# Odd layer of a two-layer decoder trunk: attention stores issued from ScalarE's queue, the merges' loads from GpSimd's

## The chip, the cores and the metric

The program runs on one core of one Trainium2 chip. The metric is the device time of one execution in microseconds, as the median of several runs; lower is better. In the profile the engines are PE (TensorE matmul), PEld (its weight loads), DVE (VectorE), ACT (ScalarE), POOL (GpSimd) and SP (SyncE). A row such as SPq, ACTq or POOLq belongs to the instruction queue of that engine: a wait, or the issue of a DMA.

## What is computed

The reference is a trunk of two residual layers over 1024 tokens of width 1024, each followed by a gated feed-forward block with a short convolution. The first layer mixes tokens by a gated delta rule and by pooling. The second one, the odd layer, is the one at hand: attention in three groups, each with eight heads of 128 channels, and each group looking back over another dilation.

```python
DIL_PATTERNS = ((128, 1), (512, 4), (2048, 16))
def odd_mixer(h, w_in, w_out, q_norm, k_norm):
    for gi, (window, dil) in enumerate(DIL_PATTERNS):
        proj = (h @ cols).reshape(B, T, 3, ATT_HEADS, ATT_DH)
        q = rms_norm(proj[:, :, 0], q_norm) * (ATT_DH ** -0.5)
        k = rms_norm(proj[:, :, 1], k_norm)
        o, lse = dilated_band_attention(q, k, proj[:, :, 2], dil, window // dil, slopes)
    wts = jax.nn.softmax(jnp.stack(lses), axis=0)
    o = jnp.sum(wts[..., None] * jnp.stack(outs), axis=0)
    return o.reshape(B, T, ATT_W) @ w_out
```

So each head has three outputs, one of each group, and they are merged by weights that come from the three softmax denominators. The merged heads are then multiplied by the output matrix.

## The kernel before, in words

All matmuls of weights are done in three passes: a weight and an activation are each split into a high part (whi, hh, oh) and a low part (wlo, hl, ol), and three products are summed in PSUM. A weight is loaded as a granule of 128 x 512 floats into a tile `raw` (4 buffers) from the sync queue at L190; ACT copies it to `whi` and another engine subtracts to get `wlo` (L185 and L186; 9 buffers of each). The subtraction runs on DVE in most of the odd layer, and on GpSimd after `lo_eng` is set back, which is ahead of the output projection.

The odd layer is written as two streams. `dense()` is the projections: for each of 12 pairs of heads (`todo`: a group g and a head pair hp) it multiplies by eight granules of q and k weights, in four blocks of 256 tokens, and, for every second pair, by eight granules of v weights. `v` goes to DRAM and comes back by strides: the stores (L1495) and loads (L1463, L1466, L1469) are issued from GpSimd. Behind the last pair it does the output projection, `update()` over two pairs of rows of the output matrix (L212 to L214 on TensorE, then L249 on DVE, which adds into the residual tile `xr`), and the first steps of the next stage.

`chains()` is everything with a chain of dependences: `attend(i)` for each pair, and `merge(hp)`. `weave()` puts them between the dense matmuls, some 1.3 to 3.5 us of dense matmuls after each step. The order of the code is a priority, and a scheduler at build time lays out each engine's queue from it; on the chip each engine's queue then runs in that order, and an instruction that waits holds up all behind it on the same queue.

In `attend(i)` a unit is a block of 256 tokens and one head: scores (PE, L1550), bias and maximum (DVE, L1562, L1566 or L1570, L1573), exponential (ACT, L1575), transposes (PE, L1583), their copy out of PSUM (ACT L1587 or DVE L1585 in turn), the product with v (PE, L1594), and the copy of the result into `stg` (ACT, L1596). After every second unit two DMAs store `stg` into the group's DRAM tensor `os` (L1600), 130 KB each: 96 in all.

In `merge(hp)`, `load(t)` brings 128 tokens of two heads from the three groups into `ld` (L1630, three DMAs of 130 KB, 3 buffers of `ld`), computes weights (DVE and ACT, L1632 to L1640) and mixes (ACT L1645, DVE L1647): 96 DMAs in all. `turn_o` transposes (PE, L1653); for hp 0 and 1 ACT copies the tile out (L1657) and two DMAs store it to `osp2` (L1659, 16 in all), from where it comes back later as a granule; for hp 2 and 3 it is split where it is.

L1600, L1630 and L1659 stand on the sync queue, beside the weights (L190), the reload of the residual tiles (`xr<-xs`, L424) and of `osp2` (L456).

Of the kernel before, what the change touches and what calls it, by code (L numbers as in the profile page):

```python
# [17 lines left out]
P = 128  # L18
# [16 lines left out]
def trunk(ctx, tc, x, c, ada_w, ada_b, norm_mix, norm_ffn, ev_w_in, ev_w_out, gdn_conv_w,  # L35
          gdn_a_log, gdn_dt_bias, gdn_norm, pool_w, pool_scale, od_w_in, od_w_out,
          att_q_norm, att_k_norm, ffn_w_up, ffn_conv_w, ffn_conv_b, ffn_w_down, out):
    nc = tc.nc
# [373 lines left out]
    osp2 = dram.tile([4, P, T], F32, name="osp2")  # L412
# [921 lines left out]
    def odd(xt, h, vec, acc):  # L1334
# [5 lines left out]
        with tc.tile_pool(name="po", bufs=1) as po:  # L1340
# [189 lines left out]
            def attend(i, need):  # L1530
# [58 lines left out]
                def values(n):  # L1589
                    b2, hh = un[n]  # L1590
                    ps = s_ps()
                    for j, (ks, a0, m) in enumerate(spans[n][0]):
                        for c, kb in enumerate(ks):
                            nc.tensor.matmul(ps[:, j * P:(j + 1) * P], pTs[n][:, a0 + c * P:a0 + (c + 1) * P],  # L1594
                                             vb(kb, hh), start=(c == 0), stop=(c == len(ks) - 1))
                    nc.scalar.copy(stg[b2][:, :, hh, 0:P], ps[:, :256].rearrange("p (a f) -> p a f", a=2))  # L1596
                    if hh:
                        for j in range(2):
                            rows = tok_rows(osc[g], g, b2 * 2 + j)
                            nc.sync.dma_start(rows[:, hp * 2:hp * 2 + 2, :], stg[b2][:, j])  # L1600

                for n in range(9):
                    if n < 8:
# [11 lines left out]
            def merge(hp, need):  # L1615
# [11 lines left out]
                def load(t):  # L1627
                    ld = et("ld", 3, (P, 3, 2, 130))
                    for g in range(3):
                        nc.sync.dma_start(ld[:, g], osc[g][t * P:(t + 1) * P, hp * 2:hp * 2 + 2, :])  # L1630
                    mx, e, dn = et("mx", 2, (P, 1, 2)), et("me", 2, (P, 3, 2)), et("dn", 2, (P, 3, 2))
                    nc.vector.tensor_reduce(out=mx[:, 0, :], in_=ld[:, :, :, 128].rearrange("p g x -> p x g"),  # L1632
                                            axis=mybir.AxisListType.X, op=ALU.max)
                    nc.vector.tensor_tensor(out=e, in0=ld[:, :, :, 128], in1=mx.to_broadcast([P, 3, 2]), op=ALU.subtract)
                    nc.scalar.activation(e, e, AF.Exp)
                    nc.vector.tensor_tensor(out=dn, in0=e, in1=ld[:, :, :, 129], op=ALU.mult)
                    nc.vector.tensor_reduce(out=mx[:, 0, :], in_=dn.rearrange("p g x -> p x g"),
                                            axis=mybir.AxisListType.X, op=ALU.add)
                    nc.vector.reciprocal(mx, mx)
                    nc.vector.tensor_tensor(out=e, in0=e, in1=mx.to_broadcast([P, 3, 2]), op=ALU.mult)  # L1640
                    if t % 2 == 0:
                        mos[t // 2] = t2k()
                    for hh in range(2):
                        m = blk4(mos[t // 2])[hh * 2 + t % 2]
                        nc.scalar.activation(m, ld[:, 0, hh, 0:P], AF.Copy, scale=e[:, 0, hh:hh + 1])  # L1645
                        for g in (1, 2):
                            nc.vector.scalar_tensor_tensor(out=m, in0=ld[:, g, hh, 0:P], scalar=e[:, g, hh:hh + 1],  # L1647
                                                           in1=m, op0=ALU.mult, op1=ALU.add)

                def turn_o(t2):  # L1650
# [4 lines left out]
                    if hp < 2:  # L1655
                        og = t2k()
                        nc.scalar.copy(og, ps)  # L1657
                        for hh in range(2):
                            nc.sync.dma_start(osp2[hp * 2 + hh][:, s], og[:, hh * 256:(hh + 1) * 256])  # L1659
                        return  # L1660
                    for hh in range(2):
                        split(o[hh][0][:, s], o[hh][1][:, s], ps[:, hh * 256:(hh + 1) * 256], nc.vector)
# [112 lines left out]
```

## Time and profile before

| | us |
|---|---|
| median of 3 runs | 3056.04 (3054.67 to 3056.47) |
| the profiled execution | 3055.07 |
| its span, first to last instruction | 3053.3 |
| TensorE busy in the span | 2965.5 (97%) |
| VectorE / ScalarE / GpSimd busy | 1938.5 / 1125.9 / 996.0 |

The span is 1.75 us shorter than the time of the same execution. The odd layer's attention runs from about 1311 us to 2300 us of the span. A row of the stretches gives, for a piece of the span, its length and then the busy time of PE, PEld, DVE, ACT and POOL (with the number of instructions), the granted clock, the mean busy share of the 16 DMA engines and the GB/s that they moved; the difference between its length and TensorE's busy time is what TensorE stood still, and the granted clock tells how much of the time it had its full rate (1.00 is 2.4 GHz, 0.50 is 1.2 GHz). A row of the waits says which instruction waited, for which one, how long in all, how many times, and how long the longest.

### The profile page before, as it was taken

What the parts mean: (1) busy time and instruction counts of PE and PEld (TensorE: products, weight loads), DVE (VectorE), ACT (ScalarE), POOL (GpSimd) and SP (SyncE); (2) the same over time, 40 slices, a digit from 0 to 9 for tenths busy, and PEclk for the clock granted to TensorE, in tenths of its full rate; (3) what the DMA queues carried; (4) which work ended last, traced back from release to release, by engine and by line L of the source; (5) the groups of instructions that cost most, each with busy time, mean ns of one, the idle gap of its engine ahead of it and who ended that gap; (6) DMA issues with size and microseconds to landing.
All of it is one profiled execution on the core that took longest, in us unless ns stands there. A gap on an engine that the chain in (4) does not pass through costs nothing.

```text
span 3053.3 us, 40242 instructions
## 1 busy us (share of the span) xinstructions
PE 2965.5 (97%) x14386; PEld 2449.4 (80%) x14386; DVE 1938.5 (63%) x3770; ACT 1125.9 (37%) x2239; POOL 996.0 (33%) x763
## 2 busy tenths in 40 slices
PE   7999999999999999999999999999999999999999
PEld 4777777778888888888888878888877788888888
DVE  6767735978887665654545636453687766666554
ACT  5434332533334433423333423333344433333210
POOL 3322223455556875200000010000032555556540
PEclk8999999999999999999999999999999999999999
DMA  7413314243433754322214232323253222224321
GB/s 255 111 46 100 90 56 152 80 152 116 131 123 98 250 152 128 133 64 74 92 61 125 68 122 63 122 61 114 68 176 117 82 85 84 84 84 162 114 90 56
DMA packets 274817, 331.46 MB, mean 109 GB/s; under 512 B 27219, under 2 KB 194234, under 8 KB 274618
## 3 DMA queue, kind: packets, MB, share of 16 engines
q1 hardware_dynamic: 266618, 300.54, 31.3%
q0 software_dynamic: 7040, 25.17, 2.4%
q10 hardware_dynamic: 960, 3.18, 0.3%
q8 instruction: 114, 1.87, 0.3%
q14 instruction: 85, 0.70, 0.1%
HBM read 251.82 MB, written 77.00 MB: 108 GB/s over the span
## 4 chain that ended last, share of the span: by engine, by line
PE 77%; DVE 5%; issue 1%; DMA 1%; ACT 1%; POOL 0%; SPq 0%; DVEq 0%; POOLq 0%; ACTq 0%
PE sp L214 12%; PE sp L212 12%; PE sp L213 12%; PE mm L1400 8%; PE mm L1398 8%; PE mm L1399 8%; PE mm L212 3%; PE mm L213 3%; PE mm L214 3%; PE sp L1594 2%; PE sp L1550 2%; PE sp L1430 1%; PE sp L1583 1%; DVE xr L1217 1%; DVE t2k L1647 0%
## 5 line engine op out<-in xcount | busy, mean ns | idle before, releaser
L1398 PE MATMUL mm<-whi,hh 128*128 128x512 f32 x1152 | 483.0, 419 | 0.0
L1400 PE MATMUL mm<-whi,hl 128*128 128x512 f32 x1152 | 453.0, 393 | 0.0
L1399 PE MATMUL mm<-wlo,hh 128*128 128x512 f32 x1152 | 451.6, 392 | 0.0
L186 POOL TENSOR_TENSOR wlo<-raw,whi 128x512 fp32r<-128x512 f32 x198 | 261.9, 1336 | 517.8 <-ACT whi L185 464.3
L246 DVE SCALAR_TENSOR_TENSOR xr<-sp,mod,xr 128x512 f32<-128x512 f32 x336 | 251.4, 750 | 183.5 <-PE sp L214 183.3
L185 ACT ACTIVATE whi<-raw 128x512 fp32r<-128x512 f32 x342 | 213.3, 629 | 322.1 <-PE sp L213 116.7
L212 PE MATMUL mm<-hh,whi 128*128 128x512 f32 x768 | 312.2, 408 | 18.3 <-DVE ft L1161 7.2
L213 PE MATMUL mm<-hl,whi 128*128 128x512 f32 x768 | 306.5, 399 | 6.7 <-DVE hl L397 6.0
L212 PE MATMUL sp<-oh,whi 128*128 128x512 f32 (+1 forms) x832 | 312.5, 376 | 0.0
L214 PE MATMUL sp<-oh,wlo 128*128 128x512 f32 (+1 forms) x832 | 310.3, 373 | 0.0
L213 PE MATMUL sp<-ol,whi 128*128 128x512 f32 (+1 forms) x832 | 310.1, 373 | 0.0
L214 PE MATMUL mm<-hh,wlo 128*128 128x512 f32 x768 | 306.0, 399 | 0.0
L186 POOL TENSOR_TENSOR wlo<-t2k,whi 128x512 fp32r<-128x512 f32 x152 | 215.4, 1429 | 163.1 <-ACT whi L185 107.2
L1495 POOL DMA_DIRECT2D vd<-v x24 | 17.6, 735 | 744.2 <-ACT v L1492 385.6
L1400 PEld LDWEIGHTS mm<-whi,hl 128*128 128x128 f32 x1152 | 216.6, 188 | 47.8
L1399 PEld LDWEIGHTS mm<-wlo,hh 128*128 128x128 f32 x1152 | 218.1, 189 | 37.0
L1398 PEld LDWEIGHTS mm<-whi,hh 128*128 128x128 f32 x1152 | 217.7, 189 | 36.1
L186 POOL TENSOR_TENSOR wlo<-wr,whi 128x512 fp32r<-128x512 f32 x108 | 168.1, 1557 | 164.3 <-ACT whi L185 157.3
L212 PEld LDWEIGHTS mm<-hh,whi 128*128 128x128 f32 x768 | 147.3, 192 | 50.2 <-issue 11.6
L214 PEld LDWEIGHTS sp<-oh,wlo 128*128 128x128 f32 x832 | 156.7, 188 | 27.5
L212 PEld LDWEIGHTS sp<-oh,whi 128*128 128x128 f32 x832 | 156.7, 188 | 27.1
L213 PEld LDWEIGHTS sp<-ol,whi 128*128 128x128 f32 x832 | 156.8, 188 | 27.0
(393 smaller groups left out, 6107.4 us busy)
## 6 DMA issues: line engine op xcount, KB each, us to landing
raw<-in_ada_w_dram SPq DMA_DIRECT2D x160, 256.0 KB
wr<-in_ffn_w_up_dram SPq DMA_DIRECT2D x72, 512.0 KB
raw<-in_od_w_in_dram SPq DMA_DIRECT2D x144, 256.0 KB
hid<-ft SPq DMA_DIRECT2D x44, 512.0 KB
raw<-in_ffn_w_down_dram SPq DMA_DIRECT2D x88, 256.0 KB
big<-hid SPq DMA_DIRECT2D x44, 512.0 KB
xr<-xs SPq DMA_DIRECT2D x32, 512.0 KB
os<-stg SPq DMA_DIRECT2D x96, 130.0 KB
```

The lines of the kernel that those rows point to most:

```text
L185: nc.scalar.activation(dst_hi, src, AF.Copy)
L186: eng.tensor_tensor(out=dst_lo, in0=src, in1=dst_hi, op=ALU.subtract)
L212: nc.tensor.matmul(ps, wh, mh, start=first, stop=False)
L213: nc.tensor.matmul(ps, wh, ml, start=False, stop=False)
L214: return nc.tensor.matmul(ps, wl, mh, start=False, stop=last)
L246: nc.vector.scalar_tensor_tensor(out=xt[o][:, s], in0=p, scalar=gate[:, o:o + 1], in1=xt[o][:, s], op0=ALU.mult, op1=ALU.add)
L1217: nc.vector.tensor_tensor(out=out, in0=x, in1=y, op=ALU.subtract)
L1398: nc.tensor.matmul(p, hh, wh, start=(k == 0), stop=False)
L1399: nc.tensor.matmul(p, hh, wl, start=False, stop=False)
L1400: nc.tensor.matmul(p, hl, wh, start=False, stop=(k == KT - 1))
L1550: nc.tensor.matmul(ps[:, at:at + len(ks) * P], qks[i][0][:, hh, blk * P:(blk + 1) * P], qks[i][1][:, hh, ks[0] * P:(blk + 1) * P], start=T ...
L1594: nc.tensor.matmul(ps[:, j * P:(j + 1) * P], pTs[n][:, a0 + c * P:a0 + (c + 1) * P], vb(kb, hh), start=(c == 0), stop=(c == len(ks) - 1))
```

## The change

The engine that issues three groups of DMAs is another one. Nothing else of the code is changed: the same bytes go to the same places.

```diff
@@ attend(): values() @@
                         for j in range(2):
                             rows = tok_rows(osc[g], g, b2 * 2 + j)
-                            nc.sync.dma_start(rows[:, hp * 2:hp * 2 + 2, :], stg[b2][:, j])
+                            nc.scalar.dma_start(rows[:, hp * 2:hp * 2 + 2, :], stg[b2][:, j])
@@ merge(): load() @@
                     for g in range(3):
-                        nc.sync.dma_start(ld[:, g], osc[g][t * P:(t + 1) * P, hp * 2:hp * 2 + 2, :])
+                        nc.gpsimd.dma_start(ld[:, g], osc[g][t * P:(t + 1) * P, hp * 2:hp * 2 + 2, :])
@@ merge(): turn_o() @@
                         for hh in range(2):
-                            nc.sync.dma_start(osp2[hp * 2 + hh][:, s], og[:, hh * 256:(hh + 1) * 256])
+                            nc.scalar.dma_start(osp2[hp * 2 + hh][:, s], og[:, hh * 256:(hh + 1) * 256])
```

The 96 stores of `stg` and the 16 of `osp2` go to ScalarE's queue, the 96 loads of `ld` to GpSimd's. The sync queue keeps the weights, the residual tiles and the reloads of `osp2`.

## Rows read from the trace of the kernel before

**Rows 1.** Stretches of the odd layer: busy time of each engine, granted clock, DMA

```profile
1311.00:1786.00 475.00, 474.81 (x2436) 397.46 (x2435) 240.88 (x700) 169.08 (x428) 13.99 (x19) 1.00 0.25 77
1786.00:1820.00 34.00, 29.88 (x127) 24.33 (x126) 16.39 (x61) 9.54 (x23) 6.49 (x9) 0.90 0.62 192
1820.00:2220.00 400.00, 399.90 (x2057) 334.67 (x2057) 216.90 (x657) 146.94 (x380) 13.14 (x17) 1.00 0.27 84
2220.00:2300.00 80.00, 71.57 (x364) 58.83 (x363) 69.09 (x196) 39.46 (x111) 25.79 (x18) 0.97 0.58 188
```

**Rows 2.** Waits of PE, 1311 to 2347 us: total, times, longest

```profile
PE mm L212 <- DVE xr L249: 4.5, 2, 4.3
PE sp L1430 <- DVE t2k L1416: 4.0, 1, 4.0
PE sp L1594 <- DVE sb L1585: 3.9, 3, 3.0
```

**Rows 3.** Waits of the sync queue, 1311 to 2347 us

```profile
SPq L1600 <- ACT stg L1596: 359.6, 41, 16.9
```

**Rows 4.** By line: count, ns minimum/median/maximum; last row: 2220 to 2300 us alone

```profile
L1600 SPq DMA_DIRECT2D os<-stg x96: 319/383/1072, 1366.1 to 2299.0; - x96
L1630 SPq DMA_DIRECT2D ld<-os x96: 319/423/1227, 1409.0 to 2302.4; - x96
L754 ACTq DMA_DIRECT2D osp<-big x4: 326/327/353, 421.3 to 489.0; - x4
L1466 POOL DMA_DIRECT2D v<-vd x16: 722/723/731, 1299.7 to 1801.5; - x16
DMA to landing us min/median/max: 3.2/6.4/7.3
L1630 SPq DMA_DIRECT2D ld<-os x35: 319/423/542, 2220.4 to 2298.1; - x35
```

**Rows 5.** Waits of ACT, 1311 to 2220 us, then of PE's weight loads, 1311 to 2347

```profile
ACT sb L1575 <- DVE neg L1573: 131.1, 50, 5.4
...
PEld sp L1594 <- ACT sb L1587: 1.8, 5, 0.4
```

**Rows 6.** DVE in order of time, 1798 to 1815 us, one of two such waits

```profile
1805.23 0.17 DVE L1632 TENSOR_REDUCE mx<-ld 128x2 f32<-128x6 f32 x1 [5.28 <-DMA ld<-os]
```

**Rows 7.** All engines in order of time, 1786 to 1816 us: the issues at 1796

```profile
1796.51 5.76 POOL L1466 DMA_DIRECT2D v<-vd  x8 [3.31 <-DMA vd<-v]
...
1797.80 2.99 SPq L1630 DMA_DIRECT2D ld<-os  x6
```

**Rows 8.** Stretches of 4 us: at the first stop, and after the second

```profile
1802.00:1806.00 4.00, 4.00 (x20) 3.29 (x20) 0.40 (x3) 0.31 (x2) 0.27 (x1) 1.00 1.05 363
...
1814.00:1818.00 4.00, 3.88 (x14) 3.23 (x14) 3.57 (x15) 0.78 (x2) 0.00 (x0) 0.50 0.37 103
```

**Rows 9.** The sync queue in order of time, 2236 to 2275 us

```profile
2250.41 0.32 SPq L1630 DMA_DIRECT2D ld<-os  x1
2262.05 0.80 SPq L1600 DMA_DIRECT2D os<-stg  x2
2262.90 0.94 SPq L1630 DMA_DIRECT2D ld<-os  x2
```

**Rows 10.** DVE in order of time, 2246 to 2254, then 2261 to 2267 us

```profile
2248.16 1.28 DVE L1410 TENSOR_REDUCE r<-t2k 128x4 f32<-128x512 f32 x2 [1.30 <-ACT t2k L1409]
...
2265.92 0.16 DVE L1632 TENSOR_REDUCE mx<-ld 128x2 f32<-128x6 f32 x1 [1.59 <-DMA ld<-os]
```

**Rows 11.** Waits of DVE, then of the sync queue, 2220 to 2300 us

```profile
DVE mx L1632 <- DMA ld<-os: 2.0, 2, 1.6
...
SPq L1630 <- DVE t2k L1647: 10.5, 5, 3.4
...
SPq L1600 <- DMA xr<-xs: 0.8, 1, 0.8
```

**Rows 12.** GpSimd in order of time, 2229 to 2300 us

```profile
2284.32 5.54 POOL L186 TENSOR_TENSOR wlo<-raw,whi 128x512 fp32r<-128x512 f32 x4 [1.35 <-ACT whi L185]
```

## The prediction, made blind

> **What bounds the kernel now.** I read the stretches of the odd layer first, then what TensorE waited for, then the chains behind each of its waits. The stretches [rows 1] show that TensorE does not stand still while the attention runs beside the projections: 474.81 of 475 us and 399.90 of 400 us are busy, at granted clock 1.00. It stands still in two places only. From 1786 to 1820 us, where the second half of the heads begins, 34 - 29.88 = 4.1 us are lost, and the clock of 0.90 costs another 3.4 us. From 2220 to 2300 us, where the last attention, two merges and the output projection fall together, 80 - 71.57 = 8.4 us are lost, and the clock of 0.97 costs 2.4 us. Both times the clock fell to its lower level behind a stop: after the first one a stretch of 4 us has 0.50, 1.2 GHz [rows 8]. So 4.1 + 3.4 + 8.4 + 2.4 = 18.3 us, or 0.6%, is about all that lies within reach here. A change of this layer can't be worth more, and it can cost more.
>
> The waits of TensorE name the two places [rows 2]: 4.0 us for `t2k` of the q and k norm (L1416), once; 4.3 us (of 4.5) for the residual update L249, once; 3.0 us (of 3.9) for the transposed probabilities (L1585), once. All three are released by DVE. None names a weight. That is the first thing to hold against the change: its aim, the sync queue, is where much waiting is seen (359.6 us in stores that wait for ScalarE's copy [rows 3]), but that queue runs so far ahead that the weights behind the stores come in time in the two long stretches.
>
> **The change part by part.**
>
> The sync queue loses 96 x 0.383 + 96 x 0.423 us = 77 us of issuing [rows 4], plus the 16 stores of `osp2`, and the waits of its stores. None of that is on the path in the two long stretches, so I count 0 there.
>
> *The stores on ScalarE.* 112 issues. The nearest rows are four DMAs that ScalarE issued in the even layer, 0.327 us each [rows 4], so 112 x 0.327 = 37 us of ScalarE, against 169.08 + 9.54 + 146.94 + 39.46 = 365 us busy of 989 [rows 1]. A pair of stores, 0.65 us, stands right behind the copy of `stg` and ahead of the next exponential. Before that exponential ScalarE waits for DVE anyway: 50 times, 131.1 us in all, 2.6 us each [rows 5]. That is the cover. The tight place is another one: TensorE's weight loads were released by ScalarE's copy of the probabilities 5 times, 0.4 us at most [rows 5]; there is no spare time there. If a pair of stores fell in front of each of those five, the cost would be 5 x 0.65 = 3.3 us. Range 0 to 3.3; I take 0, by the 50 waits, which are the place where the stores stand in the code. What is queued behind a store on ScalarE is more than the exponential: the splits of the weights (L185), the squares of the norm, the copies of v. If the store has to wait, all of these wait. One such wait is to be seen: a store of `stg` on the sync queue waited 0.8 us for a load of `xr`, whose data it has nothing to do with [rows 11], so a store can be held by somebody else's load (that the two share a completion counter is my reading). On ScalarE that is up to 0.8 us each time it happens; it was once in the 80 us of the last stretch, so it lies inside the 3.3 us.
>
> *The loads on GpSimd.* 96 issues. The nearest rows are its loads of v, 0.723 us each [rows 4]: 96 x 0.723 = 69 us. In the two long stretches GpSimd is busy 13.99 of 475 and 13.14 of 400 us [rows 1], so there is room. A load may also take longer to land from there: the v loads took 3.2 us at least [rows 4], while DVE had the loads that the sync queue had issued by 2263.84 at 2265.92 [rows 9, 10], 2.1 us. That is up to 1.1 us for each tile, and 0 where the tile is there ahead of DVE; in the long stretches I count 0 for both, and in the last one it is part of the third case below.
>
> *First stop.* The chain is: DVE stands at L1632 for a load of `ld`, 5.28 us and once more for the next tile, and L1410 of the norm comes only behind that; TensorE waits for it [rows 6, 2]. The six loads were issued on the sync queue from 1797.80, 1.3 us behind the first of eight loads of v that GpSimd began to issue at 1796.51 [rows 7], and in between the 16 DMA engines are full (share 1.05, 363 GB/s from 1802 to 1806 [rows 8]). After the change both groups are in one queue. If the `ld` loads get ahead of the v loads, which nobody waits for yet, the stop goes: -4.1 - 3.4 = -7.5 us. If they come behind all eight, the last is issued at 1796.51 + 5.76 + 6 x 0.723 = 1806.6 us, instead of 1800.8, so 5.8 us later; as the engines are emptier by then, between 0 and 5.8 us of it reaches DVE. Range -7.5 to +5.8. By the order of the issues one of the two tiles is the last of merge 0, which stands in the code before the last four v loads, and the other the first of merge 1, which stands behind them; so I take 0, one tile sooner and one later.
>
> *Last stretch.* Here the queue did hold something up. At 2250.41 the sync queue issued one load; then it stood until 2262.05, for a store that waited for ScalarE's copy of `stg`, and the two other loads of that tile, from 2262.90, and the weights behind them went out only after it [rows 9]. DVE felt it twice: it waited 2.0 us for `ld` in this stretch, 1.59 us of it at 2265.92 [rows 11, 10], and it stood 1.30 us at 2248.16 behind ScalarE [rows 10]. DVE is what TensorE waits for here, and it is busy 69.09 of 80 us [rows 1]. So of the 10.9 us in which it idled, 2.0 + 1.3 = 3.3 us can be had back, since the loads no longer stand behind the stores. If TensorE's stops shrink by as much, the lost clock shrinks in proportion: 2.4 x 3.3 / 8.4 = 0.9 us. Sum -4.2 us. The ends are -10.8 (both stops and the lost clock go) and a loss, which is the third rival below.
>
> Sum: 0 + 0 + 0 - 4.2 us. The profiled execution took 3055.07 us, 1.75 us more than its span and 0.97 us less than the median; 3055.07 - 4.2 = 3050.9 there, and 3056.04 - 4.2 = 3051.8 us for the median.
>
> **A rule that speaks against it.** The Trainium skill, "DMA: Bandwidth & Descriptors", section "Issuing engines are not separate DMA queues", says that DMAs started by several engines run on the same 16 DMA engines, and that issuing them from several engines saves only the time of the sequencer. The trace agrees that the engines are shared (the share of 1.05 above, with GpSimd's and the sync queue's loads in flight together), and by that rule alone the result is the fourth case below. What the rule leaves out is what this trace shows at 2250 us: a queue that waits holds up the DMAs behind it.
>
> **The rivals.**
>
> Second case, *all stops of the last stretch go*. For it: loads and weights stood 11.3 us behind one store (2250.73 to 2262.05 [rows 9]), and all that they feed could move forward by that. Against it: DVE is busy 86% there, and GpSimd's subtractions, on which the weights hang, stay where they are. It gives 3056.04 - 10.8 = 3045.2 us; with the first stop gone as well, 3056.04 - 18.3 = 3037.7 us.
>
> Third case, *slower: GpSimd's queue takes over the part of the sync queue*. In the last stretch GpSimd is busy 25.79 us with the low parts of the weights and activations, 1.4 us each where four stand in a row, from 2284.32 [rows 12]. It gets 35 loads [rows 4], 35 x 0.723 = 25.3 us, and the waits that go with them, for a free `ld` buffer, 10.5 us in all and 3.4 us the longest [rows 11]: together 61.6 of 80 us, in one queue in order. A low part that stands behind one tile's loads is late by 3 x 0.723 + 3.4 = 5.6 us. It decides from the point where that is more than the lead of the split over TensorE, which the nine weight buffers give. If it hits once in each of the two merges that run here, it makes 11.2 us: 3067.2 us. For it: the queue would be 77% full. Against it: GpSimd idles 54 of 80 us before, so most loads can pass while nothing stands behind them.
>
> Fourth case, *nothing that can be measured*: the waits change place, DVE stays the limit: 3056.0 us.
>
> **How the numbers follow.** About 0.2% (6.1 us) is what a measurement of this kernel can tell from no change, so faster is below 3049.9 and slower above 3062.2 us. Chances: first case 0.38, around 3051.8, of which 0.05 falls below 3049.9; second 0.27; third 0.23, of which 0.03 stays under 3062.2; fourth 0.12. So faster 0.05 + 0.27 = 0.32, slower 0.20, within 0.33 + 0.03 + 0.12 = 0.48. The range reaches from 3041 us, half-way between the two numbers of the second case, to 3067 us, the number of the third: this leaves out some 0.08 below and 0.11 above. The likeliest case's own range is 3048 to 3056.
>
> **What would show it.** The first step is right if the two long stretches keep TensorE busy within 0.5 us of their length, and wrong if TensorE's waits gain a row that is released by ScalarE (L1587 or L1575). The step on the last stretch is right if the gap of the sync queue around 2250 to 2262 is gone, DVE's wait for `ld` falls under 0.5 us there, and TensorE's idle time falls from 8.4 to about 5 us. The third case shows as waits of TensorE, or of its weight loads, for `wlo` from GpSimd, and as GpSimd's waits for DVE's L1647. At the first stop the order of the `ld` and v loads on GpSimd's queue decides, and it is read there. The prediction is wrong as a whole if the build lays out another order of the long stretches, which no row here can show.

## The result and the profile after

The changed kernel takes 3068.86 us (median of 5 runs, 3065.75 to 3070.91), the kernel before beside it 3056.47 us (5 runs): ratio 1.0041, interval 1.0029 to 1.0052. It is slower by 0.4%; the forecast was 3051.8 us. The profiled execution took 3065.75 us, its span is 3064.0 us, 10.7 us more than that of before.

The stretches of the changed kernel answer to [rows 1]. Columns: the stretch, its length, busy time (and instructions) of TensorE, its weight loads, VectorE, ScalarE and GpSimd, then the granted clock, the DMA share and GB/s.

```profile
1311.00:1786.00 475.00, 473.39 (x2424) 395.94 (x2423) 240.80 (x700) 167.90 (x428) 25.25 (x40) 1.00 0.25 77
1786.00:1820.00 34.00, 33.39 (x157) 27.33 (x156) 17.96 (x66) 11.87 (x26) 12.94 (x21) 1.00 0.63 193
1820.00:2220.00 400.00, 399.10 (x2060) 334.34 (x2059) 219.29 (x671) 148.25 (x389) 29.15 (x47) 1.00 0.28 86
2220.00:2300.00 80.00, 63.51 (x297) 51.88 (x296) 65.49 (x163) 34.01 (x95) 38.25 (x44) 0.87 0.49 167
2300.00:2347.00 47.00, 44.07 (x200) 35.63 (x200) 31.71 (x70) 13.47 (x32) 9.58 (x11) 0.97 0.28 91
```

The kernel before had, in the stretch that [rows 1] doesn't have:

```profile
2300.00:2347.00 47.00, 47.00 (x215) 38.51 (x215) 32.39 (x76) 14.13 (x31) 5.10 (x4) 0.99 0.28 94
```

The first stop is gone: 33.39 of 34 us against 29.88, and the clock is 1.00 against 0.90, which is worth 3.5 + 3.4 us. The two long stretches lose 1.4 and 0.8 us. The loss is behind 2220: TensorE stands still 16.5 of 80 us, against 8.4, at a granted clock of 0.87 against 0.97, and 2.9 of the next 47 us, where it stood still for nothing before. Idle time and lost clock overlap in part, so these terms don't add up to the 10.7 us. They do when time is counted between the same TensorE instructions of the two traces (14386 in each, in the same order but for 50 of them, in four places of the long stretches): the changed kernel then takes 1.8 us more in the first long stretch, 6.4 less at the first stop, 0.7 more in the second long stretch and 16.9 more for what ran from 2220 to 2347 us before. The rest of the program, which the change doesn't touch, was 2.4 us quicker in this execution.

TensorE's waits, 1311 to 2347 us, answer to [rows 2] (releaser, then us in total, times, longest):

```profile
PE mm L212 <- DVE xr L249: 12.4, 3, 7.5
PE sp L1594 <- ACT sb L1587: 3.9, 3, 1.8
PE sp L1594 <- DVE sb L1585: 3.0, 2, 2.6
```

The wait for the residual update L249, 4.5 us before, is now 12.4 us, and the wait for ScalarE's copy of the probabilities (L1587) is new. Neither TensorE nor its weight loads wait for `wlo` anywhere behind 2220. VectorE, which has to do L249, was late. Three places show why. First, at 2250.46 VectorE stood for a tile of `ld` ahead of L249:

```profile
2250.46 0.16 DVE L1632 TENSOR_REDUCE mx<-ld 128x2 f32<-128x6 f32 x1 [3.46 <-DMA ld<-os]
```

The sync queue, which no longer has these loads in it, had issued the eight loads of `xr` (512 KB each) at 2238.40. GpSimd issued that tile's three loads at 2242.15 and, behind a subtraction, from 2243.96, while the DMA share was 0.95 to 1.02, and they landed 5.5 to 6.0 us after their issue, against 2.3 us at the least and 3.1 us at the median. The sync queue, then GpSimd, in order of time:

```profile
2238.40 4.08 SPq L424 DMA_DIRECT2D xr<-xs  x8
```

```profile
2242.15 0.55 POOL L1630 DMA_DIRECT2D ld<-os  x1 [1.31 <-DMA xr<-xs]
2242.72 1.30 POOL L186 TENSOR_TENSOR wlo<-raw,whi 128x512 fp32r<-128x512 f32 x1
2243.96 1.08 POOL L1630 DMA_DIRECT2D ld<-os  x2
2245.06 1.27 POOL L186 TENSOR_TENSOR wlo<-raw,whi 128x512 fp32r<-128x512 f32 x1
2253.98 1.61 POOL L1630 DMA_DIRECT2D ld<-os  x3 [7.65 <-issue]
2263.52 0.54 POOL L1630 DMA_DIRECT2D ld<-os  x1 [7.92 <-issue]
...
2286.83 1.07 POOL L1630 DMA_DIRECT2D ld<-os  x2 [9.25 <-ACT stg L1596]
2287.91 1.30 POOL L186 TENSOR_TENSOR wlo<-raw,whi 128x512 fp32r<-128x512 f32 x1
2289.15 0.55 POOL L1630 DMA_DIRECT2D ld<-os  x1
2289.72 5.01 POOL L186 TENSOR_TENSOR wlo<-raw,whi 128x512 fp32r<-128x512 f32 x4
```

Second, GpSimd stands 7.65, 7.92 and 9.25 us with a load at the head of its queue. The last row names ScalarE, which was done at 2285.94; the buffer that the load needs came free with VectorE's L1647 at 2286.30. Third, what VectorE did while GpSimd ran the bottom of that fence:

```profile
2285.70 0.60 DVE L1647 SCALAR_TENSOR_TENSOR t2k<-ld,me,t2k 128x128 f32<-128x128 f32 x2
...
2287.83 7.06 DVE L1647 SCALAR_TENSOR_TENSOR t2k<-ld,me,t2k 128x128 f32<-128x128 f32 x1 [0.85 <-ACT t2k L1645]
```

One multiply-add of 128 x 128, which takes 0.34 us elsewhere, took 7.06 us. It began while GpSimd was issuing the second load and ended with GpSimd's last subtraction. I call this a hold: VectorE counts as busy, but gets on with nothing. Before, four subtractions stood in a row as well, with no load between them [rows 12], and of the operations that are short elsewhere the longest beside them took 1.26 us, about one subtraction. The Trainium skill, "SBUF — State Buffer", section "SBUF: two separate sides", says that a VectorE instruction with two inputs in SBUF and a GpSimd instruction that reads SBUF contend for one pair of ports under an exclusive lock: whichever starts first has it for its whole instruction, and the other is blocked. The trace agrees in so far as L1647, which was held, has two inputs in SBUF, while L249, with one in PSUM, took 1.26 to 1.29 us in every kernel. It differs on the rest: L1647 began 0.08 us ahead of the first subtraction, so by that rule it would have gone first, or at the worst have waited for that one subtraction, some 1.4 us.

### The profile page after: what moved, and what is told of

It is laid out like the page before. It is cut to its first block, busy times and chain, and to the rows that moved or that the text cites. A ratio compares the mean times of both kernels' runs of the same rounds, so it can differ in the third digit from the quotient of the medians.

```text
span 3064.0 us, 40197 instructions
## 1 busy us (share of the span) xinstructions
PE 2965.5 (97%) x14386; PEld 2448.6 (80%) x14386; DVE 1947.3 (64%) x3770; ACT 1125.0 (37%) x2239; POOL 1047.3 (34%) x859
## 5 line engine op out<-in xcount | busy, mean ns | idle before, releaser
L186 POOL TENSOR_TENSOR wlo<-raw,whi 128x512 fp32r<-128x512 f32 x198 | 262.9, 1341 | 433.4 <-ACT whi L185 370.9
L185 ACT ACTIVATE whi<-raw 128x512 fp32r<-128x512 f32 x342 | 213.1, 629 | 320.9 <-PE sp L213 115.0
L186 POOL TENSOR_TENSOR wlo<-t2k,whi 128x512 fp32r<-128x512 f32 x152 | 215.0, 1427 | 164.0 <-ACT whi L185 125.2
L1630 POOL DMA_DIRECT2D ld<-os x96 | 51.6, 543 | 633.7 <-DMA os<-stg 385.6
L186 POOL TENSOR_TENSOR wlo<-wr,whi 128x512 fp32r<-128x512 f32 x108 | 167.8, 1554 | 163.8 <-ACT whi L185 154.1
L212 PEld LDWEIGHTS mm<-hh,whi 128*128 128x128 f32 x768 | 146.5, 191 | 51.7 <-issue 12.7
L213 PEld LDWEIGHTS mm<-hl,whi 128*128 128x128 f32 x768 | 146.4, 191 | 40.3 <-DVE hl L397 9.2
```

Of the source, the lines that this page charges most:

```text
L185: nc.scalar.activation(dst_hi, src, AF.Copy)
L186: eng.tensor_tensor(out=dst_lo, in0=src, in1=dst_hi, op=ALU.subtract)
L212: nc.tensor.matmul(ps, wh, mh, start=first, stop=False)
L213: nc.tensor.matmul(ps, wh, ml, start=False, stop=False)
L1630: nc.gpsimd.dma_start(ld[:, g], osc[g][t * P:(t + 1) * P, hp * 2:hp * 2 + 2, :])
```

## The experiments

Theory A: the loads on GpSimd cost the time. Theory B: the stores on ScalarE do. Theory C: the sync queue, emptied, sends the `xr` loads into the merges' loads. All ratios are to the kernel before, run beside each on the same chip; where `sync` stands for a queue, it is as before. Merge 0 to 3 are the values 0 to 3 of `hp` in the diff.

| Run | Loads of merges 0, 1 / 2 / 3 | Stores | us | Ratio and interval |
|---|---|---|---|---|
| changed | GpSimd / GpSimd / GpSimd | ScalarE | 3068.9 | 1.0041 [1.0029, 1.0052] |
| e1 | sync / sync / sync | ScalarE | 3057.9 | 1.0006 [0.9996, 1.0016] |
| e2 | GpSimd / GpSimd / GpSimd | sync | 3062.9 | 1.0025 [1.0016, 1.0035] |
| e3 | GpSimd / sync / sync | ScalarE | 3057.0 | 1.0002 [0.9993, 1.0012] |
| e4 | sync / GpSimd / GpSimd | ScalarE | 3068.4 | 1.0042 [1.0026, 1.0058] |
| e5 | GpSimd / sync / sync | sync | 3051.7 | 0.9987 [0.9978, 0.9996] |
| e6 | GpSimd / ScalarE / ScalarE | ScalarE | 3054.5 | 0.9995 [0.9986, 1.0004] |
| e7 | GpSimd / GpSimd / sync | ScalarE | 3056.9 | 1.0007 [0.9997, 1.0016] |
| e8 | GpSimd / sync / GpSimd | ScalarE | 3066.7 | 1.0035 [1.0021, 1.0048] |

**Each half of the change alone.** e1 has the stores on ScalarE, e2 the loads on GpSimd:

```
-  nc.sync.dma_start(rows[...], stg[b2][:, j])       # e1: nc.scalar
-  nc.sync.dma_start(osp2[hp * 2 + hh][:, s], ...)   # e1: nc.scalar
-  nc.sync.dma_start(ld[:, g], ...)                  # e2: nc.gpsimd
```

> Only the stores (stg and osp2) go to ScalarE's queue; the merges' loads stay on the sync queue. Theory A (the loads on GpSimd cost it: they stand among GpSimd's subtractions, land late and keep DVE out): TensorE's idle time from 2220 to 2350 us is about that of before (8 to 10 us against 19 in the changed kernel), time 3047 to 3058 us. Theory B (the stores on ScalarE cost it: ScalarE's copies and exponentials come late): as slow as the changed kernel, 3064 to 3071 us, with waits of TensorE for ScalarE (L1587). Theory C (the sync queue, freed of the stores, issues the eight loads of xr earlier and into the loads of ld): slow as well, 3062 to 3070 us, with DVE waiting 3 us or more for ld behind the xr loads.

> Only the merges' loads go to GpSimd's queue; all stores stay on the sync queue. Theory A: the whole loss is here, 3064 to 3072 us, with DVE waiting 5 us or more for ld after 2220 us and single DVE instructions of 2 to 7 us beside GpSimd's subtractions. Theory B: as before, 3053 to 3059 us. Theory C: the xr loads go out some us earlier, as the sync queue is free of the ld loads, half of the loss, about 3062 us.

e1 can't be told from no change, so theory B falls as the main cause. e2 is slower, with the changed kernel's long wait for L249 in its trace:

```profile
PE mm L212 <- DVE xr L249: 10.9, 4, 7.5
```

Its 3062.9 us lie just under theory A's range and at theory C's number, so e2 doesn't part these two. The two halves make 0.06% and 0.25% against 0.41% for the whole, a difference inside the intervals.

**The loads by half of the heads.** e3 puts `(nc.gpsimd if hp < 2 else nc.sync)` into the changed kernel's load, e4 the opposite.

> The changed kernel, but the loads of merges 2 and 3 (the last stretch) stay on the sync queue; those of merges 0 and 1 are on GpSimd's, the stores on ScalarE's. Theory A: the gain at the first stop (about 7 us: 3.6 us of idle TensorE and 3.4 us of clock) stays and the loss goes, 3045 to 3053 us. Theory B: the loss stays, 3064 to 3070 us. Theory C: between, 3055 to 3063 us.

> The changed kernel, but the loads of merges 0 and 1 stay on the sync queue; those of merges 2 and 3 are on GpSimd's, the stores on ScalarE's. Theory A: the loss of the last stretch is there in full, and the first stop comes back if it was the loads on GpSimd that removed it: 3068 to 3078 us; if the stores leaving the sync queue removed it, 3064 to 3071 us. Theory B and C: 3064 to 3071 us.

e4 has the whole loss, e3 none; so merges 2 and 3 lose it. e3's 3057.0 us lie in theory C's range, though, and not in theory A's, which had the gain of the first stop in it. The first stop is gone in e3 and there in e4, but the times don't show it: e3 is 0.04% under e1, and the changed kernel 0.01% under e4, both inside the noise. The stretches 1786 to 1820 of e3 and of e4:

```profile
1786.00:1820.00 34.00, 33.38 (x155) 27.33 (x154) 17.41 (x58) 12.07 (x25) 13.22 (x22) 1.00 0.66 205
```

```profile
1786.00:1820.00 34.00, 30.59 (x137) 24.87 (x136) 17.45 (x69) 9.42 (x23) 6.49 (x9) 0.95 0.56 171
```

The gain that the forecast put into the last stretch is in neither of the runs that left the loads of merges 2 and 3 on the sync queue and moved the stores: TensorE is busy 70.22 (e1) and 69.11 (e3) of the 80 us from 2220, against 71.57 before.

**The winning half alone, and the losing half on a third queue.** e5 is the kernel before with `(nc.gpsimd if hp < 2 else nc.sync)` for the load; e6 the changed kernel with `(nc.gpsimd if hp < 2 else nc.scalar)`.

> The kernel before, with the loads of merges 0 and 1 alone issued from GpSimd; every store and the loads of merges 2 and 3 stay on the sync queue. The runs so far gave the stop at 1786 to 1820 away wherever these loads were on GpSimd, and kept it wherever they were not; the loss lay behind 2220. Theory A (the loads of merges 2 and 3 on GpSimd cost the last stretch, nothing else of the change costs anything): the first stretch 1786 to 1820 is full (33.4 us or more, against 29.9 us), the last one as before (71.6 us of 80), so the time is 3 to 7.5 us under the kernel before, a ratio of 0.9975 to 0.9990. Rival G (what is won in the first stretch is given back behind it, as TensorE was 3 to 4 us short in the long stretches of the run with the stores on ScalarE and these loads on GpSimd): a ratio of 0.9995 to 1.0010.

> The changed kernel, with the loads of merges 2 and 3 issued from ScalarE's queue instead of GpSimd's; the sync queue has weights and xr alone, as in the changed kernel. It tells apart what GpSimd has to do with the loss. Theory A (GpSimd's own queue and its subtractions beside VectorE are the cost): GpSimd is free of the loads in 2220 to 2310, so the time goes to that of the run with merges 0 and 1 alone on GpSimd, 3055 to 3059 us, unless ScalarE's queue has the same fault. Theory C (the sync queue, freed of the loads, sends the eight xr loads 5 us earlier into the loads of the last merges, whichever queue these are on): the time stays at 3066 to 3070 us, with VectorE's waits for ld tiles in 2220 to 2310 at 6 us or more. Rival S (a load that waits for VectorE's L1647 now holds up ScalarE's exponentials and copies): slower than the changed kernel, above 3070 us, with TensorE's waits for ScalarE's L1587 and L185 above 10 us against 4 us.

e5 is faster than the kernel before, as theory A has it: the gain in the first stop is real, 3.8 us by the medians. The end of its interval just reaches rival G's values. e6 decides against theory C: the sync queue is as free as in the changed kernel (the `xr` loads leave at 2242.6 us, in an execution that came to the first stop 5.6 us later), and yet the loss is gone by the time of ten runs. VectorE's waits for `ld` behind 2220 are still 6.5 us in its trace. That trace is of the slowest of the ten, 3061.4 us, where the others took 3055.7 us or less; what ran from 2220 to 2347 before takes 7.4 us more in it, against 16.9 in the changed kernel. So it is GpSimd, not the emptied sync queue, and not the late tiles alone. Rival S did not come: TensorE's waits for L1587 and L185 are 3.2 and 1.2 us, under the 10 us that it asked for.

**Which merge.** e7 is the changed kernel with merge 3's loads on the sync queue (`hp < 3`), e8 with merge 2's.

> The changed kernel, with the loads of merge 3 (from about 2253 us on) back on the sync queue; those of merges 0 to 2 stay on GpSimd. Theory A, in its two halves: the 7.5 us stop at 2245 (a tile's loads of merge 2, landed 5.5 to 6.0 us after their issue beside the xr loads) stays, what lies behind 2253 goes back to the kernel before, about 5 us: 3062 to 3065 us. If the loss is all in merge 3: 3056 to 3059 us; if it is all in merge 2: 3067 to 3070 us.

> The changed kernel, with the loads of merge 2 (to about 2245 us) back on the sync queue; those of merges 0, 1 and 3 stay on GpSimd. The xr loads stand behind the last loads of merge 2 again, and leave at about 2243 to 2245 instead of 2238. Theory C and the first half of theory A (the 7.5 us stop comes from merge 2's last loads beside the xr loads): the stop at 2245 goes, 7 to 9 us with its clock: 3059 to 3062 us. If the loss is in merge 3's loads on GpSimd: 3066 to 3070 us.

The loss is mostly merge 3's: 1.0041 to 1.0007 is 10 us, and e8 keeps nearly all of it. I had expected a half each. Between the same TensorE instructions, what ran from 2220 to 2347 before takes 4.0 us more in e3, 6.7 in e7, 11.5 in e8 and 16.9 in the changed kernel. The 7.6 us stop at 2245 is still there in e7 (it goes in e8, to 4.3 us) and costs little, some 2 us by the two ratios. What e8 still has, and e7 has not, is the held multiply-add:

```profile
2288.04 7.89 DVE L1647 SCALAR_TENSOR_TENSOR t2k<-ld,me,t2k 128x128 f32<-128x128 f32 x3 [0.51 <-ACT t2k L1645]
```

(Of these three the first took 7.37 us.) In e7 no load stands ahead of the same subtractions, and of the operations that are short elsewhere none takes more than 1.25 us beside them:

```profile
2284.87 1.28 POOL L186 TENSOR_TENSOR wlo<-raw,whi 128x512 fp32r<-128x512 f32 x1 [10.38 <-ACT whi L185]
2286.57 7.54 POOL L186 TENSOR_TENSOR wlo<-raw,whi 128x512 fp32r<-128x512 f32 x5 [0.42 <-ACT whi L185]
```

**Without the waits on GpSimd.** Theory P: the loads wait for a buffer, the subtractions pile up behind them, and then run back to back and hold VectorE. Theory L: it is the issues between the subtractions and the later landing. e9 gives merge 3 four more buffers in the changed kernel, e10 in e5:

```
+  spare = [et("qkT", 4, (P, 2, T)) for _ in range(2)]        # hp == 3
+  spare = [q[:, a, :780].rearrange(...) for q in spare for a in range(2)]
-  ld = et("ld", 3, (P, 3, 2, 130))
+  ld = spare[t - 3] if hp == 3 and 3 <= t < 7 else et("ld", 3, (P, 3, 2, 130))
```

> The changed kernel with four more ld buffers for merge 3 (in the two qkT tiles that the last attention leaves free), so that tiles 3 to 6 of merge 3 need not wait for the multiply-adds (L1647) of an earlier tile. It takes away what GpSimd's queue waits for, not the queue. Theory P (merge 3's loads on GpSimd cost the time because they wait for a buffer at the head of GpSimd's queue, 8.1 and 11.7 us, and hold back the subtractions behind them, which then run back to back and hold one operation of VectorE for 7.06 us): these waits go, no single operation of VectorE takes more than 2.5 us in 2253 to 2330, and the time goes to 3054 to 3059 us, as with merge 3's loads on the sync queue. Theory L (the cost lies in the issue on GpSimd itself, 24 x 0.54 us between the subtractions, and in the later landing): it stays at 3064 to 3069 us.

> The same four ld buffers in the kernel that has merges 0 and 1 alone on GpSimd (3051.7 us). Here the loads of merge 3 stand on the sync queue, where they waited for L1647 with weights behind them. If the prediction's step for the last stretch was right (3.3 us of VectorE's idle time hang on ld tiles that come late through the sync queue, 0.9 us of clock with them): 3047 to 3050 us. If VectorE's own work sets the last stretch and its waits move about: 3050.5 to 3053 us, no difference. Rival T (seven loads leave at once, land beside the weights and the xr loads, and put these late): above 3053 us.

e9: 3064.1 us, 1.0025 [1.0014, 1.0036], still slower, and in theory L's range. The wait for a buffer ahead of these subtractions is gone, the hold is not, so theory P fails in this part:

```profile
2292.79 1.29 POOL L186 TENSOR_TENSOR wlo<-raw,whi 128x512 fp32r<-128x512 f32 x1 [10.84 <-ACT whi L185]
2294.03 0.55 POOL L1632 DMA_DIRECT2D qkT<-os  x1
2294.60 4.97 POOL L186 TENSOR_TENSOR wlo<-raw,whi 128x512 fp32r<-128x512 f32 x4
```

VectorE has operations of 5.58, 4.18 and 3.78 us here; the first began at 2294.15, again during the issue of a load that has subtractions behind it. e10: 3050.2 us, 0.9981 [0.9972, 0.9990], against 0.9987 of e5; the intervals overlap.

**Without the subtractions on GpSimd.** e11 is the changed kernel, e12 the kernel before, both with

```
-                lo_eng[0] = nc.gpsimd      # ahead of reload(xs[1]): the 20 subtractions stay on VectorE
```

> The changed kernel with the 20 weight subtractions of the output projection (L186, wlo) left on VectorE instead of GpSimd. VectorE gets 20 x 0.69 = 14 us more work in the last stretch, so it should be slower than the changed kernel or the same; it counts beside the same edit of the kernel before. Theory P (subtractions held back on GpSimd's queue, and VectorE held by them): GpSimd has nothing left that holds VectorE or that can be held back there, so the two edited kernels differ by under 4 us, against 11 to 13 us unedited. Theory L (late issue and landing of the loads): they still differ by 8 us or more.

> The kernel before with the 20 weight subtractions of the output projection on VectorE: the ground against which the same edit of the changed kernel is read. VectorE's 14 us more in a stretch in which it is busy 69 of 80 us: 3058 to 3070 us. Theory P: within 4 us of the edited changed kernel; theory L: 8 us or more below it.

e11 takes 3049.8 us, 0.9974 [0.9964, 0.9984]; e12 takes 3046.4 us, 0.9965 [0.9954, 0.9977]. They differ by 3.4 us, where the unedited ones differ by 12.4: without subtractions on GpSimd the loads there cost little, whatever they wait for and whenever they land. That is theory P's side, under 4 us. What neither theory had: both are faster than the kernel before, although VectorE has 13 us more to do. The multiply-adds of the last merges in the kernel before, the changed kernel, and e12, from 2200 to 2347 us (count, then busy us and mean ns of one):

```profile
L1647 DVE SCALAR_TENSOR_TENSOR t2k<-ld,me,t2k 128x128 f32<-128x128 f32 x64 | 25.8, 448 | 0.7 <-ACT t2k L1645 0.4
```

```profile
L1647 DVE SCALAR_TENSOR_TENSOR t2k<-ld,me,t2k 128x128 f32<-128x128 f32 x64 | 30.8, 523 | 2.2 <-ACT t2k L1645 2.0
```

```profile
L1646 DVE SCALAR_TENSOR_TENSOR t2k<-ld,me,t2k 128x128 f32<-128x128 f32 x64 | 20.9, 372 | 1.0 <-ACT t2k L1644 0.9
```

The same 64 operations take 25.8, 30.8 and 20.9 us. Over all of VectorE's operations from 2200 to 2345 us, the time above the median of the same line and tiles, where it is over 0.3 us, sums to 13.6 us before, 19.5 us in the changed kernel, 3.5 us in e11 and 2.1 us in e12. So before the change GpSimd already took from VectorE 11.5 of the 13 us that it saved it, and the change made that worse by 5.9 us. The sum is not the loss, though. It is 17.5 us in e1 and 17.4 in e3, which can't be told from no change, so it must count where the standing falls. And 11.5 against 13 us does not by itself make e12 10 us faster; its build lays VectorE's queue out anew, and what of the gain is due to that is open.

**An issue ahead of each subtraction, and nothing else.** All traces up to here agree on one thing: every operation of VectorE of over 2.6 us behind 2220 (7.06, 7.43, 7.37, 5.58, 4.18, 3.78, 3.65 and 2.92 us) began during the issue of a load on GpSimd with a subtraction behind it. Beside issues with no subtraction within 0.2 us, operations are not longer (160 in the changed kernel from 1320 us on, 0.007 us more on the mean). Theory Q: this position is the cause. e15 puts an idle transfer of one column there, into the kernel before; e16 puts it behind the subtraction. The order of all else, on all engines, is that of the kernel before.

```
         nc.scalar.activation(hi, raw, AF.Copy)
+        nc.gpsimd.dma_start(idle[:, n:n + 1], hi[:, :1])      # e15, output projection's weights alone (abridged)
         lo_eng[0].tensor_tensor(out=lo, in0=raw, in1=hi, op=ALU.subtract)
+        nc.gpsimd.dma_start(idle[:, n:n + 1], hi[:, :1])      # e16
```

> The kernel before with 20 idle DMA issues on GpSimd, one directly ahead of each weight subtraction of the output projection (it copies one column of the high part to a scratch tensor; nobody reads it, nothing of the computation changes). There are no loads of the merges on GpSimd, no waits for a buffer, no late landing. In the traces so far every hold of VectorE above 2.5 us (7.06, 7.43, 7.37, 5.58, 4.18, 3.78, 3.65, 2.92 us) belongs to an operation that started during a load's issue on GpSimd with a subtraction right behind it; operations beside an issue with no subtraction near are not longer at all (171 in the changed kernel, 0.008 us more on the mean). Theory Q (an issue directly ahead of a ready subtraction lets VectorE be held from the issue on, through that subtraction and those that follow without a gap): several holds above 1.5 us and the sum of VectorE's excess in 2200 to 2345 at 18 us or more, against 13.6 us; time 3059 to 3068 us. Theory R (the merges' loads cost by what they wait for and by landing late): 3054 to 3058 us, as the kernel before, with holds as there.

> The same 20 issues, each directly behind its subtraction, so the same time of issuing on GpSimd; an issue then mostly stands ahead of a subtraction that still waits for ScalarE. Theory Q: fewer and shorter holds than with the issue ahead, 3055 to 3060 us and below the run with the issue ahead; where subtractions follow one another at once, as at 2284 us, it may hold as well. Theory R: no difference between the two, 3054 to 3058 us.

e15 takes 3068.4 us, 1.0041 [1.0027, 1.0056]: as much as the whole loss of the change, with none of its loads or stores moved, and 0.4 us above theory Q's range. GpSimd and VectorE in e15 (L198 is L186 here, L1654 is L1647):

```profile
2291.69 0.57 POOL L196 DMA_DIRECT2D idle<-whi  x1 [9.81 <-ACT t2k L1652]
2292.28 1.30 POOL L198 TENSOR_TENSOR wlo<-raw,whi 128x512 fp32r<-128x512 f32 x1
2293.51 0.57 POOL L196 DMA_DIRECT2D idle<-whi  x1
2294.10 1.30 POOL L198 TENSOR_TENSOR wlo<-raw,whi 128x512 fp32r<-128x512 f32 x1
2295.34 0.57 POOL L196 DMA_DIRECT2D idle<-whi  x1
2295.93 1.30 POOL L198 TENSOR_TENSOR wlo<-raw,whi 128x512 fp32r<-128x512 f32 x1
```

```profile
2291.72 5.99 DVE L1654 SCALAR_TENSOR_TENSOR t2k<-ld,me,t2k 128x128 f32<-128x128 f32 x3 [0.55 <-ACT t2k L1652]
...
L1654 DVE SCALAR_TENSOR_TENSOR t2k<-ld,me,t2k 128x128 f32<-128x128 f32 x64 | 38.2, 641 | 2.7 <-ACT t2k L1652 2.6
```

Of the three operations in the first row one began at 2293.66, in an issue, and took 4.05 us. The 64 multiply-adds take 38.2 us, and VectorE's excess is 25.5 us. e16 takes 3060.7 us, 1.0017 [1.0006, 1.0027], with an excess of 17.4 us: less, and a little outside the range that theory Q gave. Theory R falls with e15. e15 and e16 have the same 20 issues and transfers, so the change of place alone is worth 7.8 us by the medians. Of the other 5 us a part can be the same thing, since an issue behind one subtraction can stand ahead of the next: e16 has one hold too, of 4.03 us. Twenty issues that nobody waits for cost as much as the change, so the place ahead of a subtraction is enough for such a loss. That it makes up all of the loss in the changed kernel is not shown: VectorE's excess grew by 5.9 us there and by 11.9 us in e15, for the same time. The late tile of merge 2 (about 2 us by e8) and the waits for a buffer (e9 is 5 us under the changed kernel by the ratios, with intervals that overlap) can have a share.

**The gains together.** e13 is e5 with the subtractions on VectorE, e14 the same with the four buffers.

> The loads of merges 0 and 1 alone on GpSimd (3051.7 us), and the 20 weight subtractions of the output projection on VectorE (3046.4 us for that edit of the kernel before). Theory P (two separate causes: a first stop that hangs on the sync queue's loads at 1797 to 1803, and GpSimd's subtractions that hold VectorE behind 2220): the gains add, ratio 0.9945 to 0.9960, about 3040 to 3045 us; against the changed kernel with the same subtractions on VectorE (3049.8 us) that says what the loads of merges 2 and 3 on GpSimd and the stores on ScalarE still cost without the subtractions, 5 to 9 us. Rival G (the gain in the first stretch is given back when the last stretch is no longer short): ratio 0.9962 to 0.9975, as without these loads on GpSimd.

> The same, with four more ld buffers for merge 3. With GpSimd's subtractions gone, VectorE is what is left in the last stretch. If the prediction's step for the last stretch was right (VectorE's idle time behind ld tiles): 1 to 3 us less than without the buffers. If VectorE's own work sets it: within 1 us of it.

e13 takes 3042.6 us, 0.9959 [0.9944, 0.9974], e14 3043.7 us, 0.9958 [0.9944, 0.9972]. Both beat both kernels; e13 is 26 us under the changed one by the medians. It lies in the range expected where the gains add, but its interval takes in rival G's values too. That the last stretch stays good is plain from the trace of e13:

```profile
1786.00:1820.00 34.00, 33.34 (x154) 27.29 (x153) 16.91 (x58) 12.26 (x26) 13.09 (x21) 1.00 0.65 204
...
2220.00:2300.00 80.00, 75.73 (x388) 62.65 (x387) 70.53 (x211) 39.80 (x110) 4.77 (x2) 0.98 0.60 197
2300.00:2347.00 47.00, 47.00 (x222) 39.03 (x221) 34.94 (x83) 19.04 (x39) 8.05 (x6) 1.00 0.31 103
```

The four buffers bring nothing once VectorE is not held.

## Why the prediction was wrong

*What bounds the kernel* held: most changes of time fall into the two places named and the 47 us behind the second, and VectorE is what TensorE mostly waits for there. The limit of 18.3 us to what can be won held too (e13 wins 12.7 us); "it can cost more" was given too little of the chance.

*The stores on ScalarE*, counted 0, range 0 to 3.3 us: right by the time. An issue took 0.327 us at the median, as taken; e1 came 1.8 us slower by its ratio, which can't be told from 0. By the signs that the prediction named the step was not right: TensorE is 1.6 and 0.9 us short of the two long stretches, where 0.5 us was allowed, and 1.2 and 0.5 us short in e1. The other sign, TensorE waiting for L1587, appeared too, 3.9 us, and 2.1 us in e1; but e2, whose stores stay on the sync queue, has 3.7 us of it, so that row does not tell of the stores. The build did change TensorE's order in the long stretches, which the prediction feared, in four places by a few matmuls each; e2, without any such change, also lost 1.6 us in the first long stretch, so that is not what cost there.

*The loads on GpSimd*, counted 0: the step that failed. Those of merge 3 alone cost 10 us (the changed kernel against e7). The price of an issue was too high (0.538 us here, against 0.723), and what it was charged to was wrong, GpSimd's own time. What counted was the place of an issue ahead of a subtraction and the time that VectorE then stands still. The third case, given 0.23, had the engine, the stretch and GpSimd's waits for L1647 right, and its 3067.2 us are 1.7 us from the measured time; but its mechanism is not the one that ran. It had TensorE short of `wlo`; TensorE never waited for one. That its 5.6 us for a tile's loads are near the 7.06 us of the hold is chance, and it was not one hit in each of the two merges: e7 and e8 show merge 3 with 10 us, merge 2 with about 2.

The argument against the third case was that GpSimd idles 54 of 80 us. Idle time says nothing where an engine excludes its neighbour: VectorE's operations of 1.25 and 1.26 us beside the four subtractions of [rows 12] (L1573 and L1634, 0.16 and 0.17 us elsewhere) were in the trace of before and were not read. With them, VectorE's busy time from 2200 to 2345 would have been seen to hold 13.6 us of standing, and the subtractions, not the sync queue, would have been the place to look.

*First stop*, counted 0, range -7.5 to +5.8: in the range, but 6.4 us were won there between the same TensorE instructions, and 6.0 to 6.5 us in every run with these loads on GpSimd. The 4 us by which e5 is faster are less, as its trace takes 1.7 us more in the first long stretch and 2.2 more from 2220 to 2347. The loads' order came out as said, one tile between the v loads, the other behind, and neither landed sooner. GpSimd, then VectorE, in the changed kernel (the lines between are left out):

```profile
1797.13 2.89 POOL L1466 DMA_DIRECT2D v<-vd  x4 [3.77 <-DMA vd<-v]
1800.02 1.64 POOL L1630 DMA_DIRECT2D ld<-os  x3
1801.65 1.44 POOL L1466 DMA_DIRECT2D v<-vd  x2
...
1805.95 1.63 POOL L1630 DMA_DIRECT2D ld<-os  x3
```

```profile
1805.47 0.17 DVE L1632 TENSOR_REDUCE mx<-ld 128x2 f32<-128x6 f32 x1 [5.12 <-DMA ld<-os]
...
1805.76 1.27 DVE L1410 TENSOR_REDUCE r<-t2k 128x4 f32<-128x512 f32 x2
...
1811.05 0.16 DVE L1632 TENSOR_REDUCE mx<-ld 128x2 f32<-128x6 f32 x1 [0.27 <-DMA ld<-os]
```

VectorE waits for the first tile as long as in [rows 6] (5.12 us). But the norm's L1410, which stood behind the second tile at 1809.22 before, now stands ahead of it at 1805.76, so TensorE gets `t2k` 3.5 us sooner. The build laid VectorE's work out in another order; every run with merges 0 and 1 on GpSimd has this order and no stop. The order alone does not make the gain. In e1 and e4, with these loads on the sync queue, L1410 stands ahead of the second tile as well, and a stop of 3.0 and 3.1 us is left: there VectorE waited 6.67 and 6.26 us for the first tile, against 4.9 to 5.6 us with the loads on GpSimd, and L1410 came four operations later behind it. VectorE in e1:

```profile
1808.01 0.16 DVE L1632 TENSOR_REDUCE mx<-ld 128x2 f32<-128x6 f32 x1 [6.67 <-DMA ld<-os]
...
1809.39 1.27 DVE L1410 TENSOR_REDUCE r<-t2k 128x4 f32<-128x512 f32 x2
1810.58 0.15 DVE L1632 TENSOR_REDUCE mx<-ld 128x2 f32<-128x6 f32 x1
```

*Last stretch*, -4.2 us: wrong in sign. The gap of the sync queue at 2250 to 2262 did go, as said, but VectorE's wait for `ld` rose from 2.0 to 6.3 us there, and its time was never what those tiles set. e1 is the plain test of this step, as its loads stay on the sync queue and no longer stand behind the stores. The gap is gone there too:

```profile
2249.83 4.11 SPq L1630 DMA_DIRECT2D ld<-os  x3
2254.94 1.60 SPq L190 DMA_DIRECT2D raw<-in_od_w_out_dram  x2
```

VectorE's wait for `ld` fell to 1.1 us, and yet TensorE stood still 9.8 us in the 80, not 5. With four more buffers and VectorE's waits for `ld` down to 1.6 us, e10 won 1.8 us on e5 by the ratios, within both intervals, e14 nothing on e13. One term of the sum had no ground at all: the 1.30 us at 2248.16 [rows 10] were a wait for ScalarE's L1409, which ran late as ScalarE itself had stood 1.9 us for VectorE; no load of `ld` comes between.

The changed kernel can be reached from the kernel before by one edit at a time: e1, e3, e7, changed. By the ratios of about 3056 us the stores then cost 1.8 us, the loads of merges 0 and 1 win 1.2, those of merge 2 cost 1.5 and those of merge 3 cost 10.4; only the last is clear of noise. Alone, in e5, the loads of merges 0 and 1 win 4.

## What to carry to other kernels

Before moving DMAs onto GpSimd, see what stands behind them in its queue: an issue directly ahead of elementwise work that reads SBUF can hold VectorE through all of it, and nothing shows it but VectorE's own operations, which take several times their usual length and count as busy. Look for such operations first; they also show what is to be had by moving the elementwise work the other way. And try one edit stage by stage: the same loads on GpSimd won 4 us in one half of the heads (e5) and lost 12 us in the other (the changed kernel against e3).

## What the runs showed of the hardware

All of this is read from the starts and ends of operations in the traces. A VectorE operation with two inputs in SBUF that began during a subtraction of GpSimd was over when that subtraction was (2.5 us at most, beside a 128x1024 one of 2.4 us). There are two exceptions: 2.65 us in e15, through an issue and a second subtraction, and 1.92 us in e2, 1.1 us past the subtraction, through two issues behind it. One that began during a DMA issue with a subtraction directly behind it was held in 23 of 46 cases over all runs: through one subtraction or through several, over further issues of 0.55 us between them (7.06 us for five subtractions, 4.05 us for two, but 1.73 us in e15 for the first of five). The one of 7.43 us in e4 began 0.47 us ahead of its first subtraction and needs 0.35 us, so the issue itself has a part in the hold; how is not shown. Operations with one input were held as well (L1573, 1.25 us beside subtractions before; L124, 1.45 us in the changed kernel). Of 1061 with two inputs that began during an issue with no subtraction behind it, none was held. In the changed kernel GpSimd's issue took 0.538 us for `ld` and 0.724 us for v, and ScalarE's issue of a store 0.327 us at the median and 0.797 at most; GpSimd's issue of one column took 0.57 us. The same load of `ld` landed 2.3 us after its issue there, and up to 6.0 us after it beside the `xr` loads.
